# Attention in a hybrid decoder layer: the combine step queued later, six numerator buffers, single query tiles, loads per dilation, four engine orders written by hand

## The chip, the cores and the metric

The kernel runs on one core of a Trainium2 chip. The metric is the device time of one execution in microseconds (us); the time given for the kernel before is the median of three executions. PE is TensorE, DVE is VectorE, ACT is ScalarE, POOL is GpSimd, and SP is SyncE, which here only issues DMAs. POOL computes and also issues DMAs. Each engine takes its instructions in the order in which they stand in its own queue.

## What is computed

One decoder layer over 2048 positions of width 1024, in float32. One half of the layer is attention with 16 heads of 64, done three times with dilations 1, 4 and 16 and joined by the softmax of the three log-sum-exps; the other half is a state-space mixer. Both are gated, normalised, projected together and normalised again.

```python
o1, l1 = dilated_window_attention(q, k, v, slopes, DILATIONS[0])
o2, l2 = dilated_window_attention(q, k, v, slopes, DILATIONS[1])
o3, l3 = dilated_window_attention(q, k, v, slopes, DILATIONS[2])
wts = jax.nn.softmax(jnp.stack([l1, l2, l3], axis=0), axis=0)
y_att = (wts[0][..., None] * o1 + wts[1][..., None] * o2 + wts[2][..., None] * o3).astype(x.dtype)
y_att = rms_norm(y_att.reshape(Bsz, S, D_ATT) * jax.nn.silu(z_att), att_norm_g[layer])
...
mix = jnp.concatenate([y_att, y_ssm], axis=-1)
out = jnp.einsum('bse,ed->bsd', mix, w_out[layer])
x = layer_norm(alpha * x + out, ln_g[layer], ln_b[layer])
```

## The kernel before

There are three stages. From 0 to about 1265 us the input projections run with the state-space mixer woven in; from 1265 to about 1864 us the attention; from there to the end the output projection. The change touches the attention and the tiles that the output projection borrows from it.

The attention goes over 8 head pairs. A pair has 24 steps (the list `todo`, line 743): three dilations d of four groups `qd` in two halves, so step 0 to 7 is d = 0, 8 to 15 is d = 1 and 16 to 23 is d = 2. d = 0 here is dilation 16, whose windows are 128 keys wide, and d = 2 is dilation 1; except at a sequence's start, the windows of d = 1 and 2 are 256 wide. The loop of lines 747 to 772 is pipelined: in its iteration i, PE does the scores of step i, the transposes of step i-2 and the value products of step i-3. The steps of one pair run straight on into the next, so the last two steps of a pair are transposed and multiplied after the next pair's first scores.

- `load_pair` (426) makes a pair's tiles. The three mask tables `tb` and the three value tiles `v` are loaded by SP; the query tiles `qh`, `ql` and key tiles `kh`, `kl` (1 MB each) are loaded by DMAs that stand in POOL's queue (439). Query and key tiles are doubled: `qk[pr % 2]` holds one set for even and one for odd pairs.
- `permute` (460) copies the queries on POOL into the order that d = 1 (467) and d = 2 (471) want.
- `scores` (479): PE matmuls (503), then four DVE instructions per step that add the mask and take the minimum (511), then four ACT exponentials (519). `transposes` (523): PE (532), copied to `PT` by DVE (534). `values` (538): PE (552), and every second step ACT copies the result into a numerator tile `num` (557, 559, 562), of which there are four.
- `statistics` (565) and `gather` (583): when a pair's last value product is done, its row sums go by SP to DRAM (574 to 580) and back into a small tile `cm` (586).
- `combine` (588) joins the three dilations of a pair that is finished. Eight small DVE instructions and one ACT exponential on `cm` (592 to 601) give the weights; SP writes them to DRAM (602) and reads them back spread over all partitions, six DMAs into three `wb` tiles (611); POOL multiplies each numerator with its weights and adds up (613, 622), multiplies with the gate `zt` (627), and SP stores the result (628). Of pair 7 this is DVE's work. The combine of pair p is called in the steps of pair p+1, with (0, 1, 1), which is iteration 6 of that pair.

What sets the order: PE's instructions in the attention stand in the order of the code (`manual_schedule`, line 746). The other engines' and SP's are placed by a scheduler at compile time. After the attention, `load_w2`, `load_w1` and `prep_w` load the output weights into tiles that the attention no longer uses and split them; `product` multiplies.

Of the kernel before, what the change touches and what calls it, by code (L numbers as in the profile page):

```python
# [9 lines left out]
F32 = mybir.dt.float32  # L10
F32R = mybir.dt.float32r
# [7 lines left out]
NR = 16  # L19
NJ = 128  # L20
# [8 lines left out]
def hybrid_layer(ctx, tc, xT, xc, w52, wv, convw, convb, dtb, alog, dskp, gcol, wout,  # L29
# [3 lines left out]
    nc = tc.nc  # L33
# [8 lines left out]
    def dtile(name, shape):  # L42
        return dram.tile(shape, F32, name=name, tag=name)
# [6 lines left out]
    d_v = [dtile(f"d_v{d}", [16, 128, D]) for d in range(3)]  # L50
# [23 lines left out]
    with ExitStack() as c1:  # L74
# [178 lines left out]
        with tc.tile_pool(name="dtp", bufs=1, reuse_waits="tile") as dp, \  # L253
# [20 lines left out]
            h = dp.tile([128, 16, 16], F32, name="h")  # L274
# [139 lines left out]
    with ExitStack() as c2:  # L414
        qk = [c2.enter_context(tc.tile_pool(name=f"qk{i}", bufs=1, side="right", reuse_waits="tile"))
              for i in range(2)]
        stp = c2.enter_context(tc.tile_pool(name="stp", bufs=2, side="right", reuse_waits="tile"))
        cm_ = c2.enter_context(tc.tile_pool(name="cm", bufs=1, side="right", reuse_waits="tile"))
        psN = c2.enter_context(tc.tile_pool(name="psN", bufs=2, space=PSUM, reuse_waits="tile"))
        io = c2.enter_context(tc.tile_pool(name="io", bufs=1, reuse_waits="tile"))  # L420
        psS = c2.enter_context(tc.tile_pool(name="psS", bufs=4, space=PSUM, reuse_waits="tile"))
        psT = c2.enter_context(tc.tile_pool(name="psT", bufs=2, space=PSUM, reuse_waits="tile"))
        f2 = lambda a: a.rearrange("p r j -> p (r j)")
        f4 = lambda a: a.rearrange("p a b j -> p (a b j)")

        def load_pair(pr):

            A = {"pr": pr, "num": [], "tab": [], "v": [], "cur": {}}
            for d in range(3):
                tb = io.tile([128, 2, (128, 256, 256)[d]], F32, name=f"tb{d}", bufs=1)  # L430
                c0 = (512, 256, 0)[d]
                nc.sync.dma_start(tb, tabs[2 * pr:2 * pr + 2, :, c0:c0 + tb.shape[2]]
                                  .rearrange("h p c -> p h c"))
                A["tab"].append(tb)
            A["q"], A["k"] = {0: []}, []
            for x, src in (("q", d_qh), ("k", d_kh), ("q", d_ql), ("k", d_kl)):
                to = A["q"][0] if x == "q" else A["k"]
                t = qk[pr % 2].tile([128, NR, NJ], F32R, name=f"{x}{'hl'[len(to)]}")
                nc.gpsimd.dma_start(f2(t), src[pr])
                to.append(t)  # L440
            for d in range(3):
                v = io.tile([128, 16, 128], F32, name="v", bufs=3)
                nc.sync.dma_start(v, d_v[d][:, :, pr * 128:pr * 128 + 128]
                                  .rearrange("b p e -> p b e"))
                A["v"].append(v)
            A["st"] = stp.tile([128, 192], F32, name="st")
            return A

        def stat(A, k, d, h, blk):

# [9 lines left out]
        def permute(A, d):  # L460

            A["q"][d] = []
            for src in A["q"][0]:
                t, qi = io.tile([128, 16, 128], F32R, name="qp", bufs=4), src.bitcast(F32)
                for i in range(4):
                    if d == 1:
                        nc.gpsimd.tensor_copy(
                            t.rearrange("p (n b) (s j) -> p b s n j", b=4, s=4)[:, i],
                            qi.rearrange("p (b s) (n j) -> p b s n j", b=4, n=4)[:, i])
# [68 lines left out]
        def values(A, d, qd, half, pts):  # L538

            if half == 0:  # L540
                if qd == 0:
                    A["num"].append(cm_.tile([128, NR, NJ], F32, name="num", bufs=4))
                A["N"] = psN.tile([128, 512], F32, name="N")
            nm, num, v = A["N"], A["num"][d], A["v"][d]
            for b in range(2):
                bq = 2 * half + b
                blk = 4 * qd + bq
                f = first(d, qd, bq)
                kb = blk - 4 if d == 1 else blk - 1
                for k, which in ((blk, 1),) if f else ((kb, 0), (blk, 1)):  # L550
                    for h in range(2):
                        nc.tensor.matmul(nm[64 * h:64 * h + 64, bq * 128:bq * 128 + 128],  # L552
                                         v[:, k, 64 * h:64 * h + 64], pts[which][:, h, b],
                                         start=(f or not which), stop=bool(which))
            if half == 1:
                if d == 0:
                    nc.scalar.copy(f2(num[:, 4 * qd:4 * qd + 4, :]), nm)
                elif d == 1:
                    nc.scalar.copy(num.rearrange("p (b s) j -> p b s j", b=4)[:, :, :, 32 * qd:32 * qd + 32],
                                   nm.rearrange("p (b s j) -> p b s j", b=4, s=4))  # L560
                else:
                    nc.scalar.copy(num.rearrange("p r (n j) -> p n r j", j=8)[:, 4 * qd:4 * qd + 4],
                                   nm.rearrange("p (b r j) -> p b r j", b=4, r=16))
# [65 lines left out]
                              u.rearrange("p (n t) -> p n t", t=128))  # L629


        ring = {"qp": (io, 4), "v": (io, 3), "num": (cm_, 4), "wb": (cm_, 3)}
        ring.update({f"{x}{p}{i}": (qk[i], 1) for x in "qk" for p in "hl" for i in range(2)})
        W, SP, u7, free, os_ = {}, {}, [], [], []

        def big(name, dt=F32R):
            pool, n = ring[name]
            return f2(pool.tile([128, NR, NJ], dt, name=name if n > 1 else name[:2], bufs=n))

        def prep_w(e, raw, name, eng):  # L640

# [48 lines left out]
        UT = ["v", "v", "kl1"]  # L690
        banks = [("S", psS), ("S", psS), ("S", psS), ("S", psS), ("T", psT), ("T", psT)]

        def product(n, br):
# [80 lines left out]
        r0 = big("kl0", F32)  # L774
# [108 lines left out]
```

## Time and profile before

| | |
|---|---|
| median of three executions | 2262.6 us (2258.39 to 2266.82) |
| the profiled execution | 2261.54 us |
| its span, first to last instruction | 2259.7 us |
| PE busy | 2176.9 us, 96% of the span |
| DVE, ACT, POOL busy | 1142.9, 871.2, 754.1 us |
| mean granted TensorE clock | 0.966 |
| scores of pair 0 begin, of pair 7 begin | 1265.43 us, 1787.62 us |

A row of the timeline gives start and duration in us, the engine, the line, the operation, the tiles out<-in, their shape and how many are merged; in brackets the time that the engine stood idle just before, and what ended it. A row of the windows gives, for a stretch of time, its length, the busy time of PE, PE's weight loads, DVE, ACT and POOL, and last the granted clock, the share of the DMA engines that is busy, and GB/s.

### The profile page before, as it was taken

How to read it: one execution, taken by the hardware profiler on the slowest of the kernel's cores; microseconds unless marked ns; L12 is line 12 of the kernel's file. 1: busy time of each engine (PE TensorE's matmuls, PEld its weight loads, DVE VectorE, ACT ScalarE, POOL GpSimd, SP SyncE). 2: the span in 40 equal slices, each digit the busy share in tenths (PEclk: the TensorE clock that was granted, in tenths of full speed). 3: DMA queues.
4: the chain of work that ended last, by engine and by line, in shares of the span. 5: the costliest groups of instructions: out<-in, count | busy, mean ns of one | idle time of the engine just before them, and what ended most of it. 6: DMA issues, size and time to landing. Idle time of an engine off the chain costs nothing. (4 is left out here: it accounts for less than half of the span.)

```text
span 2259.7 us, 36859 instructions
## 1 busy us (share of the span) xinstructions
PE 2176.9 (96%) x13968; PEld 1815.1 (80%) x13968; DVE 1142.9 (51%) x2931; ACT 871.2 (39%) x2318; POOL 754.1 (33%) x511
## 2 busy tenths in 40 slices
PE   8999999999999999999999998889889989899998
PEld 8999888888888888888888787677777767688886
DVE  3000365562004455545434287767767886855553
ACT  4101122213112232323454376667666774322221
POOL 3100011010113555555555214446435763222121
PEclk9999999999999999999999798889888999999999
DMA  8544222222226455555543735756674656423220
GB/s 286 167 142 125 79 68 82 75 66 80 84 71 208 163 195 179 173 178 173 179 138 108 275 108 159 202 161 180 175 205 140 169 144 207 161 99 101 79 84 28
DMA packets 232449, 321.69 MB, mean 142 GB/s; under 512 B 27088, under 2 KB 166736, under 8 KB 224080
## 3 DMA queue, kind: packets, MB, share of 16 engines
q1 hardware_dynamic: 227664, 285.78, 41.5%
q0 software_dynamic: 4608, 33.56, 4.2%
q8 instruction: 110, 1.80, 0.3%
q14 instruction: 67, 0.55, 0.1%
HBM read 205.65 MB, written 113.64 MB: 141 GB/s over the span
## 5 line engine op out<-in xcount | busy, mean ns | idle before, releaser
L109 PE MATMUL pp<-xh,whi 128*128 128x512 f32 x1408 | 550.1, 391 | 0.0
L110 PE MATMUL pp<-xl,whi 128*128 128x512 f32 x1408 | 549.5, 390 | 0.0
L111 PE MATMUL pp<-xh,wlo 128*128 128x512 f32 x1408 | 548.7, 390 | 0.0
L519 ACT ACTIVATE P<-P,st 128x256 f32<-128x256 f32 (+1 forms) x768 | 345.2, 451 | 122.2 <-DVE st L511 122.0
L511 DVE CUSTOM_DVE_ANT_0 P<-S,tb 128x256 f32<-128x256 f32 (+1 forms) x768 | 234.7, 360 | 152.9 <-PE S L503 108.7
L111 PEld LDWEIGHTS pp<-xh,wlo 128*128 128x128 f32 x1408 | 264.4, 188 | 55.0
L109 PEld LDWEIGHTS pp<-xh,whi 128*128 128x128 f32 x1408 | 264.4, 188 | 54.8
L110 PEld LDWEIGHTS pp<-xl,whi 128*128 128x128 f32 x1408 | 264.5, 188 | 54.2
L99 POOL TENSOR_TENSOR wlo<-wraw,whi 128x1024 fp32r<-128x1024 f32 x44 | 106.0, 2409 | 490.0 <-ACT whi L98 490.0
L552 PE MATMUL N<-PT,v 128*64 128x128 f32 x2400 | 192.3, 301 | 49.1 <-DVE PT L534 24.1
L552 PEld LDWEIGHTS N<-PT,v 128*64 128x64 f32 x2400 | 140.9, 148 | 86.8 <-DVE PT L534 27.3
L534 DVE COPY PT<-T 128x512 f32<-128x512 f32 (+1 forms) x304 | 196.7, 676 | 2.8 <-PE T L532 2.7
L532 PE MATMUL T<-ident,P 128*128 128x128 f32 x1200 | 189.6, 298 | 7.6 <-ACT P L519 3.7
L532 PEld LDWEIGHTS T<-ident,P 128*128 128x128 f32 x1200 | 138.2, 149 | 32.9 <-ACT P L519 5.3
L519 ACT ACTIVATION_READ_ACCUMULATOR P<-P,st 128x1 f32 x768 | 144.0, 187 | 0.0
L613 POOL TENSOR_TENSOR wb<-num,wb 128x2048 f32<-128x2048 f32 x21 | 95.3, 4550 | 144.9 <-DMA wb<-d_wd 73.4
L126 DVE SCALAR_TENSOR_TENSOR ev<-pp,ev 128x512 f32<-128x512 f32 x64 | 44.1, 688 | 195.8 <-ACT ev L125 194.8
L503 PE MATMUL S<-kh,qp 64*128 64x256 f32 (+1 forms) x1024 | 140.6, 332 | 0.0
L503 PEld LDWEIGHTS S<-kh,qp 64*128 64x128 f32 x1024 | 99.7, 212 | 25.9 <-issue 24.3
L361 DVE TENSOR_SCALAR mt<-csb,cs 128x128 f32<-128x128 f32 x256 | 72.3, 353 | 74.9 <-DMA csb<-d_cs 74.9
L152 PE MATMUL pp<-vh,xh 128*128 128x384 f32 (+1 forms) x304 | 95.0, 320 | 5.5 <-ACT xh L182 5.4
L98 ACT CAST whi<-wraw 128x1024 fp32r<-128x1024 f32 x44 | 46.0, 1046 | 137.6 <-PE pp L110 134.6
(281 smaller groups left out, 3753.1 us busy)
## 6 DMA issues: line engine op xcount, KB each, us to landing
v<-d_v SPq DMA_DIRECT2D x24, 1024.0 KB
wb<-d_wd SPq DMA_DIRECT2D x48, 512.0 KB
wraw<-w SPq DMA_DIRECT2D x44, 512.0 KB
csb<-d_cs SPq DMA_DIRECT2D x32, 512.0 KB
d_v<-vt SPq DMA_DIRECT2D x64, 192.0 KB
d_za<-ev SPq DMA_DIRECT2D x32, 256.0 KB
d_xs<-cvo SPq DMA_DIRECT2D x8, 1024.0 KB
d_zs<-ez SPq DMA_DIRECT2D x8, 1024.0 KB
```

The lines of the kernel that those rows point to most:

```text
L99: nc.gpsimd.tensor_tensor(lo, raw, hi.bitcast(F32), op=OP.subtract)
L109: nc.tensor.matmul(ps, hi[:, k, :], h, start=(k == 0), stop=False)
L110: nc.tensor.matmul(ps, hi[:, k, :], l, start=False, stop=False)
L111: nc.tensor.matmul(ps, lo[:, k, :], h, start=False, stop=(k == 7))
L152: nc.tensor.matmul(ps, h, vw[k][0], start=(k == 0), stop=False)
L503: nc.tensor.matmul(ov(sp[h][:, 256 * b:256 * b + w]), A["q"][d][x][hr, blk], kv(A["k"][y][hr]), start=(m == 0), stop=(m == 2))
L511: nc.vector.tensor_tensor_reduce(P[:, h, b, 256 - w:256], sp[h][:, c0:c0 + w], tab[:, h, tab.shape[2] - w:], 1.0, 3.0e38, OP.add, OP.min, ...
L519: nc.scalar.activation(p, p, AF.Exp, bias=stat(A, 0, d, h, blk), scale=-1.0, accum_out=stat(A, 1, d, h, blk))
L532: nc.tensor.transpose(tp[:, h, b], P[:, h, b, 128 * which:128 * which + 128], ident)
L534: nc.vector.tensor_copy(pt[:, :, bl[0]:2], tp[:, :, bl[0]:2])
L552: nc.tensor.matmul(nm[64 * h:64 * h + 64, bq * 128:bq * 128 + 128], v[:, k, 64 * h:64 * h + 64], pts[which][:, h, b], start=(f or not whic ...
L613: eng.tensor_tensor(wb, nums[d], wb, op=OP.mult)
```

## The change

1. `combine` of the pair before is called with (0, 3, 0), iteration 9 of a pair, no longer iteration 6.
2. Six `num` tiles, not four.
3. One query tile each for `qh` and `ql`, in the pool `io`; the key tiles stay doubled.
4. Tables and values of the next pair are loaded per dilation by the new `load_dil`, when the same dilation of this pair is done. `load_pair` of the next pair, now the four query and key DMAs alone, is called with (0, 3, 1), iteration 10; it was called at the first scores of d = 1, iteration 8.
5. `manual_schedule` takes DVE, ACT and POOL too: in the attention their instructions stand in the order of the code. SP's are still placed by the scheduler.
6. The output weights go into other tiles, since the doubled query tiles are gone.

```diff
-            A = {"pr": pr, "num": [], "tab": [], "v": [], "cur": {}}
...
+            A = {"pr": pr, "num": [], "tab": {}, "v": {}, "q": {0: []}, "k": []}
             for x, src in (("q", d_qh), ("k", d_kh), ("q", d_ql), ("k", d_kl)):
                 to = A["q"][0] if x == "q" else A["k"]
-                t = qk[pr % 2].tile([128, NR, NJ], F32R, name=f"{x}{'hl'[len(to)]}")
+                t = (io if x == "q" else qk[pr % 2]).tile([128, NR, NJ], F32R, name=f"{x}{'hl'[len(to)]}", bufs=1)
                 nc.gpsimd.dma_start(f2(t), src[pr])
...
+        def load_dil(A, d):
+
+            pr = A["pr"]
+            tb = A["tab"][d] = io.tile([128, 2, (128, 256, 256)[d]], F32, name=f"tb{d}", bufs=1)
+            c0 = (512, 256, 0)[d]
+            nc.sync.dma_start(tb, tabs[2 * pr:2 * pr + 2, :, c0:c0 + tb.shape[2]].rearrange("h p c -> p h c"))
+            v = A["v"][d] = io.tile([128, 16, 128], F32, name="v", bufs=3)
+            nc.sync.dma_start(v, d_v[d][:, :, pr * 128:pr * 128 + 128].rearrange("b p e -> p b e"))
...
-                    A["num"].append(cm_.tile([128, NR, NJ], F32, name="num", bufs=4))
+                    A["num"].append(cm_.tile([128, NR, NJ], F32, name="num", bufs=6))
...
-        with tc.manual_schedule(engines={mybir.EngineType.PE}):
+        E = mybir.EngineType
+        with tc.manual_schedule(engines={E.PE, E.DVE, E.Activation, E.Pool}):
...
+                        for k in range(3):
+                            load_dil(pairs[0], k)
                         permute(pairs[0], 1)
-                    if (d, qd, half) == (1, 0, 0) and pr < 7:
-                        pairs[pr + 1] = load_pair(pr + 1)
...
-                    if (d, qd, half) == (0, 1, 1) and pr:
+                    if (d, qd, half) == (0, 3, 0) and pr:
                         combine(pairs.pop(pr - 1))
+                    if (qd, half) == (3, 1) and pr < 7:
+                        if pr + 1 not in pairs:
+                            pairs[pr + 1] = load_pair(pr + 1)
+                        load_dil(pairs[pr + 1], d)
...
-        load_w2(8, r0, "qh0", "kh0")
-        load_w2(10, r0, "ql0", "num")
-        load_w2(12, r0, "qp", "qp")
+        load_w2(8, r0, "kh_0", "num")
+        load_w2(10, r0, "num", "num")
+        load_w2(12, r0, "qh", "ql")
...
-        load_w2(14, r0, "qh1", "ql1")
+        load_w2(14, r0, "qp", "qp")
...
-        load_w1(0, "qp")
-        load_w1(1, "qp")
+        load_w1(0, "kh_1")
+        load_w1(1, "kl_1")
...
-        load_w1(2, "kh1")
+        load_w1(2, "qp")
```

Where it moves instructions. POOL's queue before, from the last steps of pair 1 into pair 2: the end of the combine of pair 0 (622, 627) stands among the permutes of pair 2 (467, 471), the key DMAs of pair 3 (439, `d_kh_79`, `d_kl_87`) and the query DMAs of pair 4 (`d_qh_64`, `d_ql_72`); the last row begins the combine of pair 1.

```order
L467 CAST qp<-qh 128x4x4x32 x4
L467 CAST qp<-ql 128x4x4x32 x4
L622 TENSOR_TENSOR wb<-wb 128x2048
L471 CAST qp<-qh 128x512 x4
L471 CAST qp<-ql 128x512 x4
L439 DMA kh<-d_kh_79 128x2048
L439 DMA kl<-d_kl_87 128x2048
L622 TENSOR_TENSOR wb<-wb 128x2048
L439 DMA qh<-d_qh_64 128x2048
L627 TENSOR_TENSOR wb<-wb 128x16x16x8
L439 DMA ql<-d_ql_72 128x2048
L613 TENSOR_TENSOR wb<-num,wb 128x2048
```

POOL's queue of the change in the steps of pair 1 (lines stand three lower than before: 610, 619 and 624 are the combine, here of pair 0, and 432 the query and key DMAs, here of pair 2).

```order
L468 CAST qp<-qh 128x512 x4
L468 CAST qp<-ql 128x512 x4
L610 TENSOR_TENSOR wb<-num,wb 128x2048 x2
L619 TENSOR_TENSOR wb<-wb 128x2048
L610 TENSOR_TENSOR wb<-num,wb 128x2048
L619 TENSOR_TENSOR wb<-wb 128x2048
L624 TENSOR_TENSOR wb<-wb 128x16x16x8
L432 DMA qh<-d_qh_62 128x2048
L432 DMA kh<-d_kh_78 128x2048
L432 DMA ql<-d_ql_70 128x2048
L432 DMA kl<-d_kl_86 128x2048
L464 CAST qp<-qh 128x4x4x32 x4
```

All six instructions of the combine now stand in one piece ahead of all four loads of the next pair; the same holds in the steps of the pairs 2 to 6. Pair 1's own loads have no combine ahead of them.

DVE's queue before, where the combine of pair 0 begins in pair 1 (511 masks, 534 copies transposes, 592 to 595 are the combine).

```order
L511 ISA st 128x1
L592 TENSOR_TENSOR mm<-cm 32x128
L534 COPY PT<-T 128x512
L593 TENSOR_TENSOR mm<-mm,cm 32x128
L595 TENSOR_TENSOR cm<-mm,cm 32x3x128
L511 ISA P,st<-S,tb_9889 128x128
```

And of the change, at the same combine (508 masks, 531 copies, 589 to 598 are the combine).

```order
L531 COPY PT<-T 128x512
L589 TENSOR_TENSOR mm<-cm 32x128
L590 TENSOR_TENSOR mm<-mm,cm 32x128
L592 TENSOR_TENSOR cm<-mm,cm 32x3x128
L594 TENSOR_TENSOR cm<-cm 32x3x128
L595 TENSOR_TENSOR mm<-cm 32x128
L596 TENSOR_TENSOR mm<-mm,cm 32x128
L597 RECIPROCAL mm<-mm 32x128
L598 TENSOR_TENSOR cm<-cm,mm 32x3x128
L508 ISA P,st<-S,tb_10378 128x256
```

The combine's first instruction stood in iteration 6, between the masks and the copy that PE's next value products need; its other seven were spread over the three iterations behind. Now all eight stand in one piece behind the copy of iteration 9.

SP's queue where the attention begins, before (432 tables; 443 values, `d_v_100` those of d = 0; 118 the last store of the projections).

```order
L432 DMA tb_9598<-tabs 128x2x256
L118 DMA d_za_99<-ev 128x512
L432 DMA tb_9600<-tabs 128x2x256
L443 DMA v<-d_v_100 128x16x128
L443 DMA v<-d_v_101 128x16x128
```

And of the change (442 tables, 444 values).

```order
L442 DMA tb_9605<-tabs 128x2x128
L444 DMA v<-d_v_100 128x16x128
L118 DMA d_za_99<-ev 128x512
L442 DMA tb_9609<-tabs 128x2x256
L444 DMA v<-d_v_101 128x16x128
```

The values of pair 0's first dilation moved ahead of the last store of the projections.

More of the change, by code (lines that the diff above doesn't have):

```diff
@@ L426, in load_pair @@
         def load_pair(pr):
-            A = {"pr": pr, "num": [], "tab": [], "v": [], "cur": {}}
[L429 to L435, printed above, removed]
+            A = {"pr": pr, "num": [], "tab": {}, "v": {}, "q": {0: []}, "k": []}
             for x, src in (("q", d_qh), ("k", d_kh), ("q", d_ql), ("k", d_kl)):
                 to = A["q"][0] if x == "q" else A["k"]
-                t = qk[pr % 2].tile([128, NR, NJ], F32R, name=f"{x}{'hl'[len(to)]}")
+                t = (io if x == "q" else qk[pr % 2]).tile([128, NR, NJ], F32R, name=f"{x}{'hl'[len(to)]}", bufs=1)
                 nc.gpsimd.dma_start(f2(t), src[pr])
                 to.append(t)
[L441 to L445, printed above, removed]
             A["st"] = stp.tile([128, 192], F32, name="st")
             return A
+        def load_dil(A, d):
[5 more added lines that the diff above has]
+            nc.sync.dma_start(v, d_v[d][:, :, pr * 128:pr * 128 + 128].rearrange("b p e -> p b e"))
         def stat(A, k, d, h, blk):
@@ L629, in combine @@
                               u.rearrange("p (n t) -> p n t", t=128))
-        ring = {"qp": (io, 4), "v": (io, 3), "num": (cm_, 4), "wb": (cm_, 3)}
-        ring.update({f"{x}{p}{i}": (qk[i], 1) for x in "qk" for p in "hl" for i in range(2)})
+        ring = {"qh": (io, 1), "ql": (io, 1), "qp": (io, 4), "v": (io, 3), "num": (cm_, 6), "wb": (cm_, 3)}
+        ring.update({f"k{p}_{i}": (qk[i], 1) for p in "hl" for i in range(2)})
         W, SP, u7, free, os_ = {}, {}, [], [], []
@@ L637, in big @@
             pool, n = ring[name]
-            return f2(pool.tile([128, NR, NJ], dt, name=name if n > 1 else name[:2], bufs=n))
+            return f2(pool.tile([128, NR, NJ], dt, name=name.split("_")[0], bufs=n))
         def prep_w(e, raw, name, eng):
@@ L688, in load_u @@
             nc.vector.reciprocal(r, r)
-        UT = ["v", "v", "kl1"]
+        UT = ["v", "v", "qp"]
         banks = [("S", psS), ("S", psS), ("S", psS), ("S", psS), ("T", psT), ("T", psT)]
@@ L770, in hybrid_layer @@
                         gather(pairs[pr])
-                    if (d, qd, half) == (0, 1, 1) and pr:
+                    if (d, qd, half) == (0, 3, 0) and pr:
                         combine(pairs.pop(pr - 1))
+                    if (qd, half) == (3, 1) and pr < 7:
+                        if pr + 1 not in pairs:
+                            pairs[pr + 1] = load_pair(pr + 1)
+                        load_dil(pairs[pr + 1], d)
         small = stp.tile([128, 192], F32, name="st")
-        r0 = big("kl0", F32)
-        load_w2(8, r0, "qh0", "kh0")
-        load_w2(10, r0, "ql0", "num")
-        load_w2(12, r0, "qp", "qp")
+        r0 = big("kl_0", F32)
+        load_w2(8, r0, "kh_0", "num")
+        load_w2(10, r0, "num", "num")
+        load_w2(12, r0, "qh", "ql")
         raw = big("v", F32)
```

## The prediction

> **What bounds the kernel now.** The page gives PE 96% of the span, but an average hides stages, so the first view is the windows: PE's gaps lie in the attention (1265 to 1864 us) and a shorter stretch behind it. In the attention the table of PE's waits names three that matter (who waited, for whom: us in total, times, longest):
>
> ```profile
> PE N L552 <- DVE PT L534: 24.1, 8, 6.8
> PE N L552 <- ACT num L559: 20.8, 6, 4.4
> PE N L552 <- DMA v<-d_v: 4.3, 1, 4.3
> ```
>
> Together 49 us. The second view is the clock: after such a gap it is granted at half, for 12 us as a rule and for 26 us at the start (length, busy time of PE, PE's weight loads, DVE, ACT, POOL; clock, DMA share, GB/s):
>
> ```profile
> 1275.00:1301.00 26.00, 24.99 (x168) 19.56 (x168) 10.48 (x59) 11.90 (x52) 1.07 (x2) 0.50 0.84 291
> 1510.00:1522.00 12.00, 11.53 (x80) 9.08 (x80) 9.47 (x44) 7.71 (x34) 1.12 (x2) 0.50 0.63 200
> 1588.50:1600.50 12.00, 12.00 (x82) 9.27 (x80) 8.39 (x40) 7.80 (x36) 1.12 (x2) 0.50 0.88 272
> ```
>
> The third is PE's timeline, for the length of a step and of a pair:
>
> ```profile
> 1339.08 0.33 PE L503 MATMUL S<-kh,qh 64*128 64x128 f32 x2
> 1576.85 0.30 PE L570 MATMUL N<-ident,st 128*64 128x128 f32 x1
> 1577.08 0.33 PE L503 MATMUL S<-kh,qh 64*128 64x128 f32 x2
> 1579.07 0.33 PE L503 MATMUL S<-kh,qh 64*128 64x128 f32 x2
> 1590.91 0.47 PE L503 MATMUL S<-kh,qp 64*128 64x128 f32 x2
> 1594.48 0.47 PE L503 MATMUL S<-kh,qp 64*128 64x128 f32 x2
> 1606.54 0.39 PE L503 MATMUL S<-kh,qp 64*128 64x256 f32 x2
> 1617.49 1.09 PE L552 MATMUL N<-PT,v 128*64 128x128 f32 x16 [3.06 <-ACT num L559]
> 1642.11 0.33 PE L503 MATMUL S<-kh,qh 64*128 64x128 f32 x2
> 1650.49 0.33 PE L503 MATMUL S<-kh,qh 64*128 64x128 f32 x2
> 1787.62 0.33 PE L503 MATMUL S<-kh,qh 64*128 64x128 f32 x2
> ```
>
> A narrow step takes 1.99 us (1577.08 to 1579.07), at half clock 3.57 (1590.91 to 1594.48). Steps 0 to 2, which still carry the last pair's wide transposes, take 8.4 together (1642.11 to 1650.49); steps 13 to 23 take 1642.11 - 1606.54 - 3.06 of waiting = 32.5. With seven narrow steps (13.9) and three of about 2.35 between, a pair without gaps takes **62 us**. It takes (1787.62 - 1339.08) / 6 = **74.8**. So 13 us a pair are to be had, if nothing else comes to bind.
>
> **Part 1: the wait for DVE goes.** Where the combine begins, DVE stands (rows of DVE and ACT, then of SP):
>
> ```profile
> 1580.95 0.69 DVE L534 COPY PT<-T 128x512 f32<-128x512 f32 x1
> 1586.39 0.28 DVE L592 TENSOR_TENSOR mm<-cm 32x128 f32<-32x128 f32 x1 [3.37 <-DMA cm<-d_st]
> 1587.50 0.55 DVE L595 TENSOR_TENSOR cm<-mm,cm 32x384 f32<-32x384 f32 x1
> 1588.08 0.52 ACT L596 ACTIVATE cm<-cm 32x384 f32<-32x384 f32 x1 [3.98 <-DVE cm L595]
> 1591.85 0.93 DVE L600 RECIPROCAL mm<-mm 32x128 f32<-32x128 f32 x1
> 1593.49 0.54 DVE L601 TENSOR_TENSOR cm<-cm,mm 32x384 f32<-32x384 f32 x1
> ```
> ```profile
> 1594.06 5.32 SPq L602 DMA_DIRECT2D d_wd<-cm  x1
> 1365.47 0.30 SPq L602 DMA_DIRECT2D d_wd<-cm  x1
> ```
>
> From the statistics' transpose on PE (1576.85) to `cm` in place (1586.39) are 9.5 us, and DVE's first combine instruction waits 3.37 of them with the copies behind it that PE needs. Called in iteration 9, it comes at 8.4 + 6 x 1.99 + 2.6 = 22.9 us after the pair's first scores (2.6: from a step's scores, 1579.07, to the end of its iteration's copy, 1581.64), while `cm` is there at 8.2 + 9.5 = 17.7. That wait is gone with 5 us to spare; the rest of DVE's order is as it was. The block of eight costs DVE about 3.7 us (four at 0.28, three at 0.55, one at 0.93) and the exponential between 0.5: 4.2 us in which no copy is made, so PE may wait about 3 us once a pair, all of it under the wait found below.
>
> **Part 2: the wait for numerators goes.** ACT cannot copy until POOL has read an old numerator. Six tiles cover two pairs, so the 20.8 us vanish. ACT's copies behind all four exponentials cost nothing: `N` has two buffers.
>
> **Part 3: the first values.** Their load no longer stands behind the last projection's store on SP, so 4.3 us of waiting and its half clock, 26 x (1 - 1.99 / 3.57) = 11.5, go: 15.8 us, once. Below, this could be 0. The other tables and values are asked for a third of a pair or more ahead; SP waiting in between for a store costs nothing that is due.
>
> **Part 4: POOL's order.** All six multiplications of the combine now stand ahead of the next pair's query and key loads. A DMA in POOL's queue waits for the arithmetic ahead of it:
>
> ```profile
> 1429.80 0.57 POOL L439 DMA_DIRECT2D qh<-d_qh  x1 [9.50 <-PE T L532]
> 1430.39 4.52 POOL L627 TENSOR_TENSOR wb<-wb 128x2048 f32<-128x2048 f32 x1
> 1434.84 0.59 POOL L439 DMA_DIRECT2D ql<-d_ql  x1
> 1379.90 4.50 POOL L613 TENSOR_TENSOR wb<-num,wb 128x2048 f32<-128x2048 f32 x1 [22.12 <-DMA wb<-d_wd]
> 1589.21 0.59 POOL L439 DMA_DIRECT2D qh<-d_qh  x1 [12.40 <-PE S L503]
> 1612.28 4.54 POOL L613 TENSOR_TENSOR wb<-num,wb 128x2048 f32<-128x2048 f32 x1 [21.95 <-ACT P L519]
> 1621.25 9.08 POOL L613 TENSOR_TENSOR wb<-num,wb 128x2048 f32<-128x2048 f32 x2
> 1630.30 9.21 POOL L622 TENSOR_TENSOR wb<-wb 128x2048 f32<-128x2048 f32 x2
> 1645.67 4.57 POOL L627 TENSOR_TENSOR wb<-wb 128x2048 f32<-128x2048 f32 x1
> ```
>
> `ql` leaves at 1434.84, just when the 4.52 us of line 627 end. Before, that cost nothing: queries were loaded two pairs ahead and keys a pair ahead. Now a pair cannot begin until this chain has run in the pair before it, from that pair's first scores:
>
> - to the combine on DVE: 22.9, and 12 x (1 - 1.99 / 3.57) = 5.3 for the half clock after the long wait: 28.2;
> - the weights on DVE and ACT: 4.2;
> - to DRAM, back spread, first multiplication: 18.2 in the pair shown (1594.03 to 1612.28), with `qh` and `ql` in flight since 1589.21; 14.4 in pair 1 (1365.47 to 1379.90) with none. Now only the 1 MB of values runs beside it: 15;
> - POOL: 4.54 + 9.08 + 9.21 + 4.57 = 27.4, the gate's load hidden behind the second half;
> - the four loads.
>
> For those four in a row the trace has the start of the attention:
>
> ```profile
> 1239.61 0.75 POOL L439 DMA_DIRECT2D qh<-d_qh  x1 [0.31 <-POOL y L383]
> 1245.84 2.29 POOL L467 CAST qp<-qh 128x512 fp32r<-128x512 f32 x4 [3.40 <-DMA qh<-d_qh]
> 1251.47 2.29 POOL L467 CAST qp<-ql 128x512 fp32r<-128x512 f32 x4 [3.35 <-DMA ql<-d_ql]
> 1239.60:1253.80 14.20, 14.20 (x65) 11.75 (x64) 0.00 (x0) 1.19 (x2) 6.97 (x13) 1.00 0.99 368
> ```
>
> The first is there after 6.2 us, the third after 11.9, all after 14.2, at 368 GB/s. The store of `d_ua` (1 MB) starts at the same moment, 3 us if it takes its full share. I take 15, between 12 and 18.
>
> The sum is 28.2 + 4.2 + 15 + 27.4 + 15 = **89.8 us** a pair, where PE has 62 + 5.3 + 3 of work: about 20 us of idle PE at each pair's start. Pair 1, which begins without a wait, takes 5.3 less, 84.5. The ends: weights 14.4 or 18.2, loads 12 or 18, half clock 12 us or up to 26 (6.2 more). The low ends give 86; the high ones 102, or 96 with any two of the three, which I take as the end.
>
> Two pages of the Trainium skill would make it shorter. "TensorE: Matmul & The Clock Gate", section "What's actually happening", has the full clock back after about 3.4 us of sustained work; then a restart would lose 1.5 us, not 5.3, and the whole would come out some 19 us lower. The windows above, half clock through 12 us of busy PE, speak against it. "DMA: Bandwidth & Descriptors", section "Anatomy of one DMA", puts a GpSimd DMA at 2.0 us plus bytes over 436 GB/s: 11.6 us for 4.19 MB, some 20 us lower in the whole; the row of 14.2 us decides.
>
> **The sum.** Pair 1 begins at 1339.1 - 15.8 = 1323.3, pair 2 at 1407.8, pair 7 at 1407.8 + 5 x 89.8 = 1856.8, which is 69 us later than 1787.6. From there I take the change as nil:
>
> ```profile
> 1834.39 1.97 PE L552 MATMUL N<-PT,v 128*64 128x128 f32 x16 [2.48 <-ACT num L559]
> 1852.62 5.06 POOL L627 TENSOR_TENSOR wb<-wb 128x2048 f32<-128x2048 f32 x1 [0.46 <-DMA wb<-d_za]
> ```
>
> Pair 7 loses this wait for numerators and that for DVE, with their half clocks, and gains a half-clock start (5.3); the output weights, one staging tile after another, stand behind the store of pair 6's combine, which ends 28.2 + 4.2 + 15 + 27.4 = 75 us into pair 7, as against 70 (1857.7) before. Take 12 us either way. So 2261.5 + 69 = **2331 us**; the profiled execution is 1 us from the median. With a cycle of 86 to 96 it is 2309 to 2367.
>
> **Rivals.** *The chain is shorter*: weights 14.4, loads 12, a restart that loses 2. Then 22.9 + 2 + 4.2 + 14.4 + 27.4 + 12 = 82.9 a pair, pair 7 at 1323.3 + 80.9 + 5 x 82.9 = 1819, in all 2293. For it speaks that in the new order less runs beside these DMAs; against it the 18.2 us of the pair shown.
>
> *Faster: the loads get past the arithmetic.* If POOL handed out the four DMAs without ending the multiplications ahead, or these came so early that the loads lie under PE's work, a pair would take 62 + 3 = 65 us, pair 7 would begin at 1323.3 + 6 x 65 = 1713, and the whole take 2187. The point from which it decides is a cycle of (1787.6 - 1323.3) / 6 = 77.4 us: below, the change wins. It needs 12 us out of the 89.8. Against it stand the rows at 1430.39 and 1434.84.
>
> *More is late*: the first values still miss (15.8 more), or the output weights come 10 to 20 us later and PE waits for them with nothing to fill: 2345 to 2365.
>
> **Chances.** The forecast 0.63, the shorter chain 0.17, more is late 0.12, faster 0.08. The range from 2275 to 2380 takes in the first three and leaves out the fast case. A measurement here can tell about 0.5%, 11 us. Faster by more: 0.08; within it, which needs a cycle of 75 to 79: 0.05, from the lower end of the shorter chain; slower: 0.87.
>
> **What would show it.** In the new profile the waits of line 552 for DVE and for numerators should all but vanish, and PE's largest wait should be the scores' for the key and query loads, six times about 20 us, at the starts of pairs 2 to 7 and not of pair 1. POOL should go from line 624 straight into the four DMAs. The starts of pairs should stand 85 to 95 us apart, with half clock behind each. Pair 1 should begin near 1323; if near 1339, part 3 failed. I am wrong if the loads leave POOL while it still multiplies, or if they leave after the combine and PE has not run out of steps by then.

## The result, and the profile after

| | before | after |
|---|---|---|
| median of four executions, us | 2263.5 (2258.4 to 2266.8) | 2339.2 (2338.5 to 2346.6) |
| ratio | | 1.034, 95% interval 1.032 to 1.037 |
| profiled execution, its span | 2261.5, 2259.7 | 2339.9, 2338.1 |
| mean granted clock | 0.966 | 0.958 |
| first scores of pairs 1, 2, 7, all keys there | 1339.1, 1412.2, 1787.6 | 1335.6, 1418.0, 1844.8 |
| from there to the end of the span | 472.1 | 493.3 |

The changed kernel is 3.4% slower. First the table of PE's waits from 1265 us on (who waited, for whom: us in total, times, longest):

```profile
PE S L500 <- DMA kh<-d_kh: 65.5, 6, 11.9
PE S L500 <- DMA kl<-d_kl: 31.1, 6, 6.0
PE N L549 <- DVE PT L531: 23.6, 7, 3.4
PE S L708 <- ACT qp L642: 20.3, 1, 20.3
```

Line 549 no longer waits for numerators or values, and for DVE 3.4 us once a pair. In their place stand 16 us a pair for the key loads, six times, and behind the attention one wait of 20 us. PE's timeline shows where (start, duration, and in brackets the idle time ahead of the row and what ended it):

```profile
1335.62 0.33 PE L500 MATMUL S<-kh,qh 64*128 64x128 f32 x2
1364.94 0.66 PE L549 MATMUL N<-PT,v 128*64 128x128 f32 x8 [3.37 <-DVE PT L531]
1412.51 0.47 PE L500 MATMUL S<-kh,qh 64*128 64x128 f32 x2 [10.43 <-DMA kh<-d_kh]
1417.96 0.47 PE L500 MATMUL S<-kl,qh 64*128 64x128 f32 x2 [4.98 <-DMA kl<-d_kl]
1503.92 0.48 PE L500 MATMUL S<-kl,qh 64*128 64x128 f32 x2 [4.90 <-DMA kl<-d_kl]
1844.81 0.48 PE L500 MATMUL S<-kl,qh 64*128 64x128 f32 x2 [5.28 <-DMA kl<-d_kl]
1979.11 2.08 PE L708 MATMUL S<-qp,v 128*128 128x512 f32 x4 [20.27 <-ACT qp L642]
```

From the moment pair 2 has its keys to the same moment of pair 3 are 1503.92 - 1417.96 = 86.0 us. The links of that chain stand in the timelines of DVE, SP and POOL (SP's rows from 1942 and POOL's from 1922 on belong to the tail):

```profile
1443.38 0.27 DVE L589 TENSOR_TENSOR mm<-cm 32x128 f32<-32x128 f32 x1
```
```profile
1445.08 0.38 SPq L444 DMA_DIRECT2D v<-d_v  x1
1447.89 0.32 SPq L599 DMA_DIRECT2D d_wd<-cm  x1
...
1942.38 0.40 SPq L658 DMA_DIRECT2D kl<-wout  x1
...
1956.84 0.30 SPq L599 DMA_DIRECT2D d_wd<-cm  x1
1958.40 3.69 SPq L608 DMA_DIRECT2D wb<-d_wd  x6
1962.18 0.53 SPq L658 DMA_DIRECT2D kl<-wout  x1
```
```profile
1458.09 4.57 POOL L610 TENSOR_TENSOR wb<-num,wb 128x2048 f32<-128x2048 f32 x1 [36.10 <-DMA wb<-d_wd]
...
1482.67 4.59 POOL L624 TENSOR_TENSOR wb<-wb 128x2048 f32<-128x2048 f32 x1
1487.19 0.60 POOL L432 DMA_DIRECT2D qh<-d_qh  x1
...
1488.82 0.57 POOL L432 DMA_DIRECT2D kl<-d_kl  x1
...
1922.14 8.98 POOL L788 TENSOR_TENSOR num<-num,wb 128x2048 f32<-128x2048 f32 x2 [6.02 <-DMA wb<-d_za]
...
1978.05 3.69 POOL L645 TENSOR_SCALAR kl<-kl,gc 128x1024 f32<-128x1024 f32 x1 [21.64 <-DMA kl<-wout]
```

The first load goes out right behind line 624. The links: 25.4 us to the combine, 4.5 for the weights, 10.2 to DRAM and back, 29.1 on POOL, 16.7 for the loads. From the windows, the clock at the attention's start, around the 3.4 us wait, and behind the start of pair 2:

```profile
1275.00:1295.00 20.00, 20.00 (x136) 15.65 (x138) 9.30 (x54) 10.84 (x48) 2.12 (x4) 0.50 0.46 156
```
```profile
1365.00:1370.00 5.00, 5.00 (x42) 4.10 (x44) 4.52 (x19) 5.00 (x20) 0.00 (x0) 0.66 0.69 158
...
1418.00:1424.00 6.00, 6.00 (x44) 5.22 (x46) 2.32 (x10) 2.23 (x9) 3.99 (x8) 0.51 0.00 0
1424.00:1430.00 6.00, 6.00 (x77) 4.99 (x76) 3.68 (x20) 3.93 (x18) 0.00 (x0) 1.00 0.02 5
```

The wait for values is gone, yet the half clock at the start came all the same, with PE busy throughout. So pair 1 began 3.5 us earlier than before, not the 15.8 forecast.

### The profile page after: what moved, and what is told of

Read it like the earlier page. It is cut to its first block, busy times and chain, and to the rows that moved or that the text cites. A ratio compares the mean times of both kernels' runs of the same rounds, so it can differ in the third digit from the quotient of the medians.

```text
span 2338.1 us, 36848 instructions
## 1 busy us (share of the span) xinstructions
PE 2165.2 (93%) x13968; PEld 1805.9 (77%) x13968; DVE 1148.9 (49%) x2931; ACT 869.0 (37%) x2318; POOL 754.3 (32%) x511
## 4 chain that ended last, share of the span: by engine, by line
PE 76%; DMA 10%; POOL 6%; DVE 3%; ACT 2%; issue 2%; SPq 1%; DVEq 0%; POOLq 0%; ACTq 0%
PE pp L110 13%; PE pp L109 13%; PE pp L111 13%; DMA kl<-d_kl 4%; DMA wb<-d_wd 3%; PE S L709 3%; PE S L500 3%; PE S L710 3%; PE S L708 3%; PE N L549 3%; PE T L529 3%; POOL wb L610 2%; PE pp L153 2%; PE pp L154 2%; PE pp L152 2%; POOL wb L619 2%
## 5 line engine op out<-in xcount | busy, mean ns | idle before, releaser
L549 PE MATMUL N<-PT,v 128*64 128x128 f32 x2400 | 184.1, 293 | 23.6 <-DVE PT L531 23.6
L549 PEld LDWEIGHTS N<-PT,v 128*64 128x64 f32 x2400 | 135.3, 143 | 59.4 <-DVE PT L531 25.3
L500 PE MATMUL S<-kh,qp 64*128 64x256 f32 (+1 forms) x1024 | 129.0, 311 | 0.0
L500 PEld LDWEIGHTS S<-kh,qp 64*128 64x128 f32 x1024 | 90.6, 192 | 23.0 <-issue 22.0
L500 PE MATMUL S<-kh,qh 64*128 64x128 f32 x256 | 42.7, 327 | 66.1 <-DMA kh<-d_kh 65.5
```

What stands on the lines that cost most here:

```text
L500: nc.tensor.matmul(ov(sp[h][:, 256 * b:256 * b + w]), A["q"][d][x][hr, blk], kv(A["k"][y][hr]), start=(m == 0), stop=(m == 2))
```

## The experiments

The theory was that POOL's order makes the stall. Its rivals: the single query tiles make it, or one of the other hand orders does; beside it, two things were unexplained, the 20 us of the tail and the half clock at the start. Ratios are to runs of the kernel before on the same chip, whose medians there were 2266 to 2269 us (2263.5 on the chip of the result). So times from different rows can differ by some us through the chip alone. Starts of pairs (all keys there) and waits are from each run's own profile.

| run | us, median | ratio to before, 95% interval | mean distance of pair starts 1 to 7 | from pair 7's start to the end |
|---|---|---|---|---|
| e1 loads ahead of the combine | 2215.3 | 0.977, 0.975 to 0.978 | 67.2 | 476 |
| e2 POOL's order by the scheduler | 2243.3 | 0.987, 0.983 to 0.990 | 69.4 | 489 |
| e3 kernel before, hand orders alone | 2299.3 | 1.014, 1.012 to 1.015 | 79.0 | 484 |
| e4 weights of block 9 on `qh` | 2320.5 | 1.023, 1.021 to 1.024 | 84.7 | 472 |
| e5 as e1, four numerators | 2273.7 | 1.003, 1.002 to 1.004 | 77.3 | 472 |
| e6 as e1, combine spread | 2220.6 | 0.981, 0.978 to 0.983 | 65.4 | 491 |
| e7 combine in iteration 6 | 2299.6 | 1.014, 1.013 to 1.016 | 79.3 | 484 |
| e8 as e1, filler at the start | 2204.6 | 0.972, 0.971 to 0.974 | 67.1 | 477 |
| e9 e4, e6 and e8 together | 2203.7 | 0.971, 0.969 to 0.974 | 65.3 | 485 |
| e10 as e9, combine in one piece | 2207.9 | 0.974, 0.973 to 0.976 | 66.9 | 479 |
| e11 as e9, block 8 off DVE | 2190.5 | 0.965, 0.964 to 0.967 | 65.2 | 471 |

### Is it POOL's order? e1, e2, e3

e1 moves the loads of the changed kernel ahead of the combine; the single query tiles stay.

```diff
-                    if (d, qd, half) == (0, 3, 0) and pr:
-                        combine(pairs.pop(pr - 1))
+                    if (d, qd, half) == (0, 3, 0) and pr:
+                        if pr < 7:
+                            pairs[pr + 1] = load_pair(pr + 1)
+                        combine(pairs.pop(pr - 1))
```

> The changed kernel, with one thing moved: the four query and key loads of the next pair stand ahead of the combine in the code (iteration 9 of a pair), not behind it, so that in POOL's order they stand ahead of its six multiplications. Theory A (POOL's order makes the stall: loads wait behind 29 us of arithmetic): the waits of PE for kh and kl (65.5 + 31.1 us before PE's six pair starts) vanish, the pair starts stand 62 + 3.4 = 65 us apart instead of 85.4, pair 7 starts near 1335.6 + 6 x 65.4 = 1728 and, with the 493 us behind that start, the whole takes about 2222 us. Theory B (the single query tiles make it: the loads cannot start before the old queries are read, wherever they stand): the starts stay 80 to 86 us apart and the time stays within 2310 to 2340. Theory C (DVE, busy 35.8 us of 40 in a stretch where PE never waits, takes over as the bound): starts 70 us apart, about 2250.

e2 gives POOL's order back to the scheduler; e3, below, is the kernel before with the hand orders alone.

```diff
-        with tc.manual_schedule(engines={E.PE, E.DVE, E.Activation, E.Pool}):
+        with tc.manual_schedule(engines={E.PE, E.DVE, E.Activation}):
```

> The changed kernel with POOL alone taken off the list of engines whose order is the code's (PE, DVE and ACT stay on it); the scheduler then puts most pairs' loads ahead of the multiplications, a few multiplications between them. Theory A (POOL's order): the waits for kh and kl nearly go, starts 65 to 72 us apart, 2222 to 2262 us. Theory B (single query tiles, or DVE's and ACT's orders): starts still 80 us or more apart, 2310 to 2340 us.

And e3:

```diff
-        with tc.manual_schedule(engines={mybir.EngineType.PE}):
+        with tc.manual_schedule(engines={mybir.EngineType.PE, mybir.EngineType.DVE, mybir.EngineType.Activation, mybir.EngineType.Pool}):
```

> The kernel before with only its list of engines changed: DVE, ACT and POOL now also follow the code's order, everything else (combine in iteration 6, four numerators, two query tiles, its loads) as before. In POOL's order the six multiplications then stand ahead of the next pair's loads. Theory A (POOL's order, by the sizes that the changed kernel showed): a chain of 17.7 to the combine, 2.7 for half clock, 4.2 for the weights, 10.2 to DRAM and back, 29.1 on POOL, 16.7 for the loads = 80.6 us a pair, pair 2 at 1339 + 78 = 1417, pair 7 at 1820, the whole about 2293 us, waits of PE for kh and kl of some 15 us at six starts. Theory B (the stall needs the single query tiles): no such waits, 2262 us within 11.

POOL's timeline of e1, in pair 2:

```profile
1420.18 0.60 POOL L432 DMA_DIRECT2D qh<-d_qh  x1 [5.17 <-PE T L529]
...
1421.81 0.57 POOL L432 DMA_DIRECT2D kl<-d_kl  x1
1445.05 4.57 POOL L610 TENSOR_TENSOR wb<-num,wb 128x2048 f32<-128x2048 f32 x1 [22.67 <-ACT num L556]
```

Before its first multiplication POOL sits idle for 22.67 us; the loads fit there, for nothing. PE's waits for `kh` and `kl` are gone from e1, pairs stand 67.2 us apart, and the time is 2215.3 where theory A said 2222; pair 7 begins 10 us later than it said (1738.1), and the stretch behind is 17 us shorter. That rules out the single query tiles as the cause: they are in e1. In e2 the scheduler puts most loads ahead of the multiplications, and PE does not wait for keys either. What is worse than in e1 is the stretch behind pair 7's start, 13 us longer, and the wait for DVE, three of them 7.6 to 8.0 us long, from the table of PE's waits of e2:

```profile
PE N L549 <- DVE PT L531: 37.6, 8, 8.0
```

And e3 makes the stall in the kernel before, doubled query tiles and all. POOL goes from line 627 straight into the loads (POOL's timeline of e3, then PE's waits):

```profile
1393.65 4.59 POOL L627 TENSOR_TENSOR wb<-wb 128x2048 f32<-128x2048 f32 x1
1398.17 0.60 POOL L439 DMA_DIRECT2D qh<-d_qh  x1
```
```profile
PE S L503 <- DMA kl<-d_kl: 31.3, 6, 6.4
PE N L552 <- DVE PT L534: 22.1, 6, 4.6
PE S L503 <- DMA kh<-d_kh: 20.0, 6, 5.2
```

2299.3 against the 2293 of theory A and the 2262 of its rival. The keys are waited for some 8.6 us a start, not 15; pairs stand 79.0 us apart, not 80.6; and the stretch behind pair 7's start is 12 us longer than before. e3 has the hand orders of DVE and ACT too. e2 has these two without POOL's, and no wait for keys; e1 has all three with the loads ahead, and none either. So the stall comes from the loads' place behind the multiplications in POOL's queue, and POOL's hand order is what puts them there.

### The later combine, the numerators: e7, e5, e6

e7 is the changed kernel with the combine back at (0, 1, 1).

```diff
-                    if (d, qd, half) == (0, 3, 0) and pr:
+                    if (d, qd, half) == (0, 1, 1) and pr:
```

> The changed kernel with the combine back in iteration 6 of a pair, the loads still behind it. Theory A (the chain from the combine to the loads sets the pair; the later combine alone lengthens it): chain 17.7 (statistics in place) + 2.7 + 4.2 + 10.2 + 29.1 + 16.7 = 80.6 us instead of 85.4, six times: about 26 us faster than the changed kernel, 2313, with PE waiting 3 to 4 us a pair for DVE's copy and less for kh and kl. Theory B (the wait for the statistics, which the later combine was to remove, costs more than the chain wins): 2340 or more.

```profile
PE S L500 <- DMA kl<-d_kl: 33.3, 6, 6.3
PE N L549 <- DVE PT L531: 21.8, 6, 4.3
PE S L500 <- DMA kh<-d_kh: 18.5, 6, 4.6
```

PE's waits of e7, above, have 47 us less for `kh` than the changed kernel, 2 more for `kl` and 2 less for DVE. It is 40 us faster, more than the 26 expected. Pairs stand 79.9 us apart from pair 2 on (theory A: 80.6), which gives 27; pair 2 has its keys 4 us earlier (1414.0), and the stretch behind pair 7's start is 9 us shorter. So the later combine was not free: its three iterations are 6 us, and with the loads behind it nearly all of them, 5.5 us a pair, came back in the next pair's start.

e5 is e1 with four numerator tiles.

```diff
-                    A["num"].append(cm_.tile([128, NR, NJ], F32, name="num", bufs=6))
+                    A["num"].append(cm_.tile([128, NR, NJ], F32, name="num", bufs=4))
...
-        load_w2(8, r0, "kh_0", "num")
-        load_w2(10, r0, "num", "num")
+        load_w2(8, r0, "kh_0", "xw")
+        load_w2(10, r0, "xw", "num")
```

> As the version with the loads ahead of the combine (2215 us), but with four numerator tiles as before, and two tiles of their own for the output weights of blocks 9 and 10. Theory A (with the combine later, six are needed): the second dilation's first copy of a pair must wait for POOL's first multiplication, which ends 42 us into the pair (1378.25 + 4.56 - 1340.90), while the copy is due some 28 us into it: about 12 to 14 us of waiting a pair on ACT's copy and PE behind it, seven times, 2290 to 2310 us. Theory B (six only save the 20.8 us that the kernel before lost to this wait): 2235 to 2245 us. Theory C (six tiles bring nothing once the loads are early): 2215 us.

The table of ACT's waits of e5 has the wait that theory A named, and at its size:

```profile
ACT num L556 <- POOL wb L610: 85.8, 7, 13.5
```

That is 12.3 us a pair on ACT, of which 10 reach the pair (77.3 against 67.2). In all 58 us: fewer than A's 75 to 95, far more than B's 20 to 30. With the combine in iteration 9 four numerators are too few. What six would save with the combine in iteration 6, where the kernel before waited 20.8 us, no run shows.

e6 is e1 with the combine's DVE work in three places.

```diff
             nc.scalar.activation(ee, ee, AF.Exp)
+            yield
             nc.vector.tensor_tensor(s_, s_, ee, op=OP.mult)
...
+            yield
             nc.vector.reciprocal(mm, mm)
...
-                        combine(pairs.pop(pr - 1))
+                        comb = combine(pairs.pop(pr - 1))
+                    if pr and (d, qd, half) in ((0, 3, 0), (0, 3, 1), (1, 0, 0)):
+                        next(comb, None)
```

> As the version with the loads ahead of the combine (2215 us), but the combine's eight DVE instructions stand in three places: three and the exponential in iteration 9, three in iteration 10, two in iteration 11. Theory A (PE's 23.6 us of waiting for DVE, 3.4 a pair, comes from the block being in one piece, and each wait is followed by some 3.6 us of half clock, a loss of 1.6): the wait falls below 1 us a pair and 25 to 35 us go: 2180 to 2190. Theory B (DVE has no room, 35.8 busy of 40 in a stretch without waits, so the same time is waited in smaller pieces): 2205 to 2215.

Neither theory held. Pair 7 begins 9.5 us earlier than in e1 (1728.7 against 1738.1), and the 14.5 us behind it are lost again. SP's queue of e6 has the tail's stall:

```profile
1837.96 0.32 SPq L601 DMA_DIRECT2D d_wd<-cm  x1
1839.52 3.69 SPq L610 DMA_DIRECT2D wb<-d_wd  x6
1845.28 0.38 SPq L660 DMA_DIRECT2D kl<-wout  x1
```

The last pair of weight blocks is loaded behind the last combine's six spread loads (0.5 MB each), and PE waits 12.2 us for it. In e1 that load goes out ahead of them, at 1846.0 against 1851.1 for the combine's store and 1853.6 for the six loads. The order of e6 is the one that the changed kernel's SP rows show too (1958.40, then 1962.18). The code there is the same: SP's order is the scheduler's, which changes with what is done elsewhere.

### The tail: e4

```diff
-        load_w2(8, r0, "kh_0", "num")
+        load_w2(8, r0, "kh_0", "qh")
...
-        load_w2(12, r0, "qh", "ql")
+        load_w2(12, r0, "num", "ql")
```

> The changed kernel with two names swapped among the tiles of the output weights: row block 9 goes to the query tile qh instead of to a numerator tile, block 12 to the numerator tile that it leaves. Theory A (the tail's 21 us come from the first round of the one staging tile, which now waits for a numerator that POOL frees only at the end of pair 6's combine, so that one round more stands behind it): PE's wait of 20.3 us for qp of line 642 goes, the span from pair 7's start to the end falls from 493 to about 472, the whole to 2318 us. Theory B (the round trip of the last combine on SP's queue holds the last round up, whatever came first): the 20.3 us stay or turn up at another line, 2335 to 2340 us.

Block 9 no longer waits for a numerator that pair 6's combine must free, and the staging tile `r0` is a round further. SP's queue of e4:

```profile
1939.39 0.38 SPq L658 DMA_DIRECT2D kl<-wout  x1
...
1960.45 0.33 SPq L599 DMA_DIRECT2D d_wd<-cm  x1
```

The last load of `r0` stands 21 us ahead of the last combine's store; the 20.3 us wait is gone, the stretch is 472 us, and the time is 2320.5 for theory A's 2318. So the tail's 21 us are the place of one 1 MB load in SP's queue. The new tile names alone don't make it: e1 has them, its load goes out in time, and its stretch is 476 us. They leave one more round of `r0` to do behind pair 6's combine, and then SP's order decides. In e2, e3 and e7 the last load goes out ahead of that store too, and the stretch is still 484 to 489 us; what holds these three up no run here shows.

### The half clock at the start: e8

```diff
+                    if i == 2:
+                        fill(3)
                     pts[i] = scores(pairs[pr], d, qd, half)
+                    if i == 2:
+                        fill(4)
...
+        def fill(n):
+            kf, ps = f2(pairs[0]["k"][0]), psN.tile([128, 512], F32, name="N")
+            for _ in range(n):
+                nc.tensor.matmul(ps, kf[:, 0:128], kf[:, 0:512], start=True, stop=True)
```

> As the version with the loads ahead of the combine (2215 us), with seven more matrix products of 128x512, whose results nobody reads, at the start of the attention: three ahead of the third step's scores and four ahead of the first transposes, where PE stands idle for 0.5 and 0.35 us before 28 us of half clock. Theory A (these short gaps start the half clock): PE stays at full clock, 28 x 0.44 = 12 us less the 1.6 us of the products: 2204 to 2207. Theory B (something else takes the clock down there): half clock from about 1271 to 1298 as without them, 2215 to 2218.

Without the seven products (e1), and with them (e8), the same window:

```profile
1275.00:1301.00 26.00, 26.00 (x190) 20.07 (x189) 13.06 (x70) 15.31 (x65) 2.12 (x4) 0.55 0.60 208
```
```profile
1275.00:1301.00 26.00, 26.00 (x315) 20.95 (x313) 22.57 (x104) 24.11 (x102) 5.04 (x10) 1.00 0.69 235
```

The clock stays full, pair 1 begins at 1323.7, not 1335.2, and the time falls by 10.8 us, as theory A said. So seven products at this place keep the half clock away. That the two short gaps alone bring it is not shown, for the products also add dense work there, and elsewhere longer gaps bring none. At the start of pair 7 e8 itself has one of 1.80 us, and the clock around it stays full (PE's timeline and the window):

```profile
1734.88 0.63 PE L529 MATMUL T<-ident,P 128*128 128x128 f32 x4 [1.80 <-ACT P L516]
```
```profile
1728.00:1754.00 26.00, 24.20 (x297) 19.39 (x295) 20.40 (x95) 20.20 (x88) 16.98 (x18) 1.00 0.41 110
```

### Together: e9, e10, e11

> Four edits together: loads ahead of the combine, seven filler products at the start, the combine's DVE work in three places, and the output weights' block 9 on the query tile. Theory A (the gains add, and the spread combine's 12 us, seen at the start of pair 7, were lost again only because the last weights' load stood behind the last combine's six loads on SP, where it now stands ahead of them): pair 7 starts at 1726.5 - 12.3 = 1714, 472 us behind it, 2188 us. Theory B (the spread itself delays the end of the attention and the last combine): 2200 to 2210.

> As the version with all four edits, but with the combine's DVE work in one piece. Theory A (the spread is worth 12 us): 2204.6 less the 4 us by which the stretch behind pair 7's start (476.5) is longer than with the weights swapped (472), so 2200 us. Theory B (the spread is worth nothing at the end): within 3 us of the version with all four.

The 12 us in both texts were misread from the second step of pair 7 in e1 (1740.98); its first row gives the 9.5 above. e9 missed: 2203.7. Pair 7 begins at 1717.3, but DVE's and PE's timelines of e9 have this behind it, and the window behind that half clock:

```profile
1721.50 3.64 DVE L650 SCALAR_TENSOR_TENSOR kh<-kl,gc,kh 128x1024 fp32r<-128x1024 f32 x1 [0.86 <-ACT kh L649]
```
```profile
1726.73 1.09 PE L529 MATMUL T<-ident,P 128*128 128x128 f32 x4 [2.79 <-ACT P L516]
```
```profile
1728.00:1754.00 26.00, 26.00 (x179) 20.32 (x179) 11.28 (x65) 14.14 (x62) 8.83 (x12) 0.50 0.21 54
```

Line 650 splits output-weight block 8. e10, which has the combine in one piece, keeps its 23.6 us of waiting. There the split takes 1.66 us, and the same window has full clock (1.00). e10 begins pair 7 8.9 us later than e9 and is 4 us slower in all, so neither of its theories held: the spread does gain at the pairs, and in e9 most of that is lost again behind pair 7's start. e11 has POOL and ACT make that half block.

```diff
-        load_w2(8, r0, "kh_0", "qh")
+        load_w2(8, r0, "kh_0", "qh", nc.gpsimd)
```

> The version with all four edits (2203.7 us), with the low half of output-weight block 8 made by POOL and ACT like its neighbour's, not by DVE. In the profile of the version with all four, one such DVE instruction of 3.64 us stands among the copies at the start of pair 7, PE waits 2.8 us behind it, and 27 us of half clock follow. Theory A (that instruction is what took the spread combine's gain back): 2.8 + 27 x 0.44 = 15 us less, 2189. Theory B (POOL's 5 us more, or the next late block, takes its place): 2198 to 2205.

The same window of e11:

```profile
1728.00:1754.00 26.00, 23.66 (x280) 18.63 (x279) 23.07 (x102) 22.91 (x92) 8.73 (x8) 1.00 0.52 132
```

Full clock, although PE stands idle twice in it, for 0.92 us (up to 1744.32) and 1.36 us (up to 1747.83); and 2190.5 us for theory A's 2189. This version beats both kernels: 3.5% faster than the one before (ratio 0.965, 0.964 to 0.967), some 149 us below the changed one's median.

## Why the prediction was right, step by step

The direction, the mechanism and its place were as forecast: loads behind POOL's arithmetic, PE idle at the starts of pairs 2 to 7. The span came out 9 us above the sum, 2338 against 2329 (the span before, 2259.7, and the 69 us forecast). That it is so close is in part luck, since four terms were off, by up to 22 us, and partly cancel:

| step | predicted | measured | off by |
|---|---|---|---|
| part 3, start of pair 1 | 15.8 us earlier | 3.5 | +12.3 |
| part 4, pair 1 | 84.5 | 82.3 | -2.2 |
| part 4, five more pairs | 89.8 each | 85.4 | -22.1 |
| pair 7 to the end | 0 | +21.2 | +21.2 |

- **Part 1** held: no wait for `cm`, and 3.4 us a pair for the block of eight where about 3 was said. What it left unsaid is that the loads come later by as much as the combine does; e7 prices this move at 40 us, 9 of them behind pair 7's start.
- **Part 2** held: the waits for numerators are gone. e5 shows that this wait would have grown with the later combine.
- **Part 3** was half right. The 4.3 us of waiting went. The step that failed is "and its half clock": the half clock was put down to this one gap, and it came without it, for some 27 us from about 1270 on. With seven more products in front of that stretch (e8) it stays away, and pair 1 begins at 1323.7; the prediction had 1323.3. What starts it there stays open: two gaps of 0.49 and 0.35 us stand before it, but longer ones in e8 and e11 bring none.
- **Part 4** was right in its mechanism, and its size is 4.4 us a pair too long. In pair 2, DRAM and back takes 10.2 and not 15. The rows it came from gave 14.4 and 18.2; in the shorter one a 1 MB load of values left SP just ahead of the six spread loads (1368.29, then 1368.72), and now it leaves ahead of the combine's store (1445.08), which may be the reason; no run tried it. The half clock loses 2.5 and not 5.3, since about half of it passes while PE still waits for `kl` (from 1412.51 to 1417.96; full clock is back at about 1424). Against that POOL takes 29.1, not 27.4, 1.6 of it a wait between the first two multiplications, and the loads 16.7, not 15. The cycle measured, 85.4, lies just under the 86 to 96 from which the time was given. That upper end was also added up wrongly: weights and loads at their high ends give 96, but either of them with the long half clock gives 99.
- **The tail** was taken as nil, 12 us either way; it is 21. The output weights were named as the place, as coming 5 us later. That the staging tile's last load can stand behind the last combine's loads on SP was not seen. That is a size outside the stated bounds, and it is what the rival "more is late" had described.
- **The rivals.** *The chain is shorter* came nearer in the cycle (its 82.9 a pair, the forecast's 89.8, measured 85.4), not in the total, where the tail and the start of pair 1 were off for both. *The loads get past the arithmetic* did not happen by itself. Where the code puts them ahead, and the start is mended (e8), its 2187 compares with 2204.6: pairs of 67.1 us and not 65, six times, since half clock follows each wait for DVE, and 4 us in the tail.

## What to carry to other kernels

Where one queue both computes and issues loads, put the loads at the first point at which their tiles are free, ahead of arithmetic that waits for something itself: here the same six multiplications a pair made a difference of some 124 us (2339.2 and 2215.3, on two chips). An order written by hand takes over every accident of the code's order, for each engine that it covers; give it to one engine at a time and look at each. After a gap is removed, look whether the clock came back with it, since something else may be holding it down.

## What the hardware showed that was not expected

- Neither the coming nor the length of half clock follows the length of the gap. Behind a wait of 3.37 us it lasts about 3.4 us (0.66 over the 5 us from 1365). That agrees with the Trainium skill, "TensorE: Matmul & The Clock Gate", section "What's actually happening", which has full clock back after one busy window of about 3.4 us. Behind 0.49 and 0.35 us at 1267 to 1269 it lasts some 27 us, with PE busy for 20.00 of 20.00 us, which that section does not give. Behind 2.79 us in e9 it lasts 26 us and more; 0.92 and 1.36 us in e11 and 1.80 in e8 bring none. What tells these apart, no run here shows.
- DVE's split of a weight block (two inputs and an output in SBUF, the on-chip memory) takes 1.27 us with POOL idle (at 1986.29 in the changed kernel), and as long beside POOL's line 645, which has one tensor as input. Begun while POOL is in a multiplication or subtraction of two tensors (lines 788 and 647), it takes 4.74 and 2.83 us (timelines of DVE and POOL of the changed kernel):

```profile
1927.46 4.74 DVE L643 SCALAR_TENSOR_TENSOR num<-kl,gc,num 128x1024 fp32r<-128x1024 f32 x1 [8.19 <-ACT num L642]
...
1933.32 1.27 DVE L643 SCALAR_TENSOR_TENSOR kh<-P,gc,kh 128x1024 fp32r<-128x1024 f32 x1
...
1936.68 2.83 DVE L643 SCALAR_TENSOR_TENSOR kl<-P,gc,kl 128x1024 fp32r<-128x1024 f32 x1
```
```profile
1931.09 3.82 POOL L645 TENSOR_SCALAR kl<-kl,gc 128x1024 f32<-128x1024 f32 x1
1936.07 2.36 POOL L647 TENSOR_TENSOR num<-kl,num 128x1024 fp32r<-128x1024 f32 x1 [1.16 <-ACT num L646]
```

The first ends at 1932.20, 1.08 us behind the end of POOL's line 788 (1922.14 + 8.98 = 1931.12). The third ends at 1939.51, again 1.08 us behind that of line 647 (1936.07 + 2.36 = 1938.43). Both seem to have waited for POOL and then run. So does the 3.64 us split of e9: it ends at 1725.14, 1.08 us behind POOL's line 631 (1719.48 + 4.58 = 1724.06). The Trainium skill, "SBUF — State Buffer", section "SBUF: two separate sides", calls the port pair of DVE and POOL an exclusive lock, held for a whole instruction. The rows beside lines 788, 647 and 631 agree with it; the one that runs at full speed within line 645 does not. No run here took POOL's work away to test it.
